# Loading the second half of the tokens behind the first quarter of the modulation, and accumulating half of its keys with the first half's

## The chip, the cores and the metric

The kernel runs on one core of one Trainium2 chip. The metric is the device time of one execution in microseconds; 1126.92 us is the median of three runs before the change.

## The reference

One layer of a diffusion backbone, in float32: 1024 latent tokens and 256 context tokens of width 1024. What matters here is its beginning. The modulation comes from the vector `c` (and `c_ctx` for the context) through the large matrix `w_mod`; the tokens are normalised, scaled and shifted with it, and then projected to keys, values and so on.

```python
mod_x = (jax.nn.silu(c) @ w_mod[l] + b_mod[l])[:, None, :]
mod_c = jax.nn.silu(c_ctx) @ w_mod[l] + b_mod[l]
sh1, sc1, gt1, sh2, sc2, gt2 = jnp.split(mod_x, N_MOD, axis=-1)
...
h_x = _modulate(x, g_pre_mix[l], sh1, sc1)    # rmsnorm(x, gain) * (1 + scale) + shift
h_c = _modulate(ctx, g_pre_mix[l], csh1, csc1)
u_x, q_x, k_x, v_x = _project(h_x, w_in[l])   # one matrix, four slices
u_c, q_c, k_c, v_c = _project(h_c, w_in[l])
attn_x = _neighbourhood_attention(q_x, k_x, v_x, k_c, v_c, rpb[l])
```

After that come the pooling mixer, the output projection and a squared-ReLU MLP, each with its own normalisation. They are the same before and after the change.

## The kernel before

**Numbers and tiles.** To keep float32's accuracy, every large product is made of three float32r matmuls: each operand is split into a high and a low part (`high_low`, `split` for weights, `modulated` for tokens), and `three` (L168 to L170) issues high by high, high by low, low by high. A page is a tile of 128 x 1024 float32, 512 KB; 33 of them are in the pool `pg`. A bank is a PSUM tile of 128 x 512; there are 8.

**The beginning.** The tokens are in two halves of 512, each in four pages with the tokens along the partitions: `xp` and `xq`. The 1024 columns of the width form eight blocks of 128, called k. For the keys, the columns must lie along the partitions, so each half is transposed by PE, block by block, into a bank (L289 for the first half, `turned`, L282, for the second). Of the modulation, shift and scale are needed here. `w_mod` is loaded in four quarters of two blocks each: four pages per quarter (`mod_load`, L244) beside one page of key weights (`wk0` to `wk3`, L148). For a quarter, `mod_rows` (L307) makes 16 matmuls that give its shift and scale as rows, which the trace shows as 32 pieces `pm`; ACT copies them, and `shift_scale` (L316, L320 to L322) turns them into columns, `a1` and `s1`.

With these, `latent(b, k, src)` modulates block k of half b, and `feature_group` adds block k to one of the key banks `pk{j}_{b}`: j counts four groups of 128 key features. A loop over the quarters q does this for the first half: modulate blocks 2q and 2q + 1 (ACT writes the high part, DVE the plain and the low one), twelve matmuls of block 2q, then the next quarter's weights and rows (`quarter(q + 1)`), then the twelve matmuls of block 2q + 1 with the next shift and scale between. In the last quarter the 16 transposes of the context (`pct`, L360) stand in place of the next rows.

**After the loop.** ACT modulates the context (`hc`, L175 and L176), copies the first half's keys out of their banks (L375), and then the second half of the tokens is normalised (`normalise("b", xq)`: squares on ACT, L130, the power -1/2 on POOL, L139, the scaling on DVE, L277). PE makes the context's keys in two groups of tokens (`pkc`); behind each group four blocks of the second half are transposed and modulated, here with `on_act=True`, where ACT writes the plain and the high part and DVE the low one. Then come all 96 matmuls of the second half's keys (8 blocks x 4 groups x 3), and their copies, L432. The value weights `wv` follow.

**What sets the order.** `in_order` ties the instructions of PE, ACT, DVE and SP in this part to the order in which they are written: no instruction of an engine passes an earlier one. All loads of the part are on SP's queue, in this order: the four pages of `xp`; per quarter one page of `wk` and four of `w_mod`; two pages of context, `cp`; four pages of `xq`. They are 26 pages, and no page of the pool is used twice among them. The value weights are released behind the last ACT and the last DVE instruction of the part (`issue_after`).

Of the kernel before, what the change touches and what calls it, by code (L numbers as in the profile page):

```python
# [17 lines left out]
P = 128  # L18
D = 1024
KT = D // P  # L20
# [59 lines left out]
def hybrid_block(ctx, tc, x, ctx_in, w_mod, b_mod, gp1, gp2, w_in, pool_w, rpb, w_out, w1, w2, vectors,  # L80
                 mask, edge, out):
    nc = tc.nc
# [9 lines left out]
    def cst(name, shape, dt=F32):  # L92
        return const.tile(shape, dt, tag=name, name=name)

    def sm(name, n, bufs=1):
        return small.tile([P, n], F32, tag=name.split("_")[0], name=name, bufs=bufs)

    def page(name, dt=F32):
        return act.tile([P, 1024], dt, tag="pg", name=name)
# [19 lines left out]
    xg, og = tiles(x), tiles(out)  # L119

    ident = cst("ident", [P, P])
# [7 lines left out]
    def mean_square(junk, src, ms):  # L129
        nc.scalar.activation(junk, src, AF.Square, scale=D ** -0.5, accum_out=ms)  # L130

    def rsqrt_of(name, ms, more=None):
        v = sm(f"v{name}", 1, 4)
        if more is None:
            nc.vector.tensor_scalar_add(v, ms, EPS)
        else:
            nc.vector.scalar_tensor_tensor(v, ms, EPS, more, add, add)  # L137
        r = sm(f"r{name}", 1, 4)
        nc.gpsimd.tensor_tensor(r, v, nhalf, ALU.pow)  # L139
        return r  # L140
# [5 lines left out]
    def load(name, src):  # L146
        raw = wraw.tile([P, 1024], F32, tag="raw", name=f"{name}w")
        nc.sync.dma_start(raw.rearrange("p (a b) -> p a b", b=src.shape[-1]), src)  # L148
        return raw

    def high_low(name, raw):
        hi = whl.tile([P, 1024], F32R, tag="hl", name=f"{name}h")
        lo = whl.tile([P, 1024], F32R, tag="hl", name=f"{name}l")
        split(raw, hi, lo)
        return hi, lo
# [4 lines left out]
    def pair(w, kk, c0, n):  # L160
        return w[2 * kk * P : (2 * kk + 2) * P, c0 : c0 + n].rearrange("(a p) f -> p a f", p=P)

    def wk(w, k, lo, c, n):
        return w[k // 2][lo][:, (k % 2) * 512 + c : (k % 2) * 512 + c + n]


    def three(ps, ahi, alo, bhi, blo, first, last, more=False):
        nc.tensor.matmul(ps, ahi, bhi, start=first, stop=False, skip_group_check=more)  # L168
        nc.tensor.matmul(ps, ahi, blo, start=False, stop=False, skip_group_check=more)  # L169
        nc.tensor.matmul(ps, alo, bhi, start=False, stop=last, skip_group_check=more)  # L170

    def modulated(tmp, name, src, scale, shift, hi, lo, n, on_act=False):
        h = tmp.tile([P, 512], F32, tag="t", name=f"{name}t")
        if on_act:
            nc.scalar.activation(h[:, :n], src, AF.Identity, bias=shift, scale=scale)  # L175
            nc.scalar.copy(hi, h[:, :n])  # L176
        else:
            nc.scalar.activation(hi, src, AF.Identity, bias=shift, scale=scale)
            nc.vector.tensor_scalar(h[:, :n], src, scale, shift, mul, add)
        nc.vector.tensor_tensor(lo, h[:, :n], hi.bitcast(F32), sub)  # L180
# [36 lines left out]
    with tc.tile_pool(name="ps1", bufs=8, space=PSUM) as ps1, tc.tile_pool(name="tmp1", bufs=3) as tmp:  # L217

        def bank(name):
            return ps1.tile([P, 512], F32, tag="mm", name=name)  # L220
# [14 lines left out]
        def token_tile(name, src):  # L235
            t = page(name)
            nc.sync.dma_start(t, src)
            return t


        def mod_load(q, kh, w):
            src = w_mod[:, w * D + q * 256 : w * D + (q + 1) * 256].rearrange("(h k p) f -> h p k f", p=P, h=2)
            t = page(f"wm{q}_{kh}_{w}")
            nc.sync.dma_start(t.rearrange("p (k f) -> p k f", k=4), src[kh])  # L244
            return t
# [3 lines left out]
        for q in range(4):  # L249
            raw_k.append(load(f"wk{q}", pair(w_in, q, 1024, 512)))  # L250
            wm.append([[mod_load(q, kh, w) for w in range(2)] for kh in range(2)])
        cp = [token_tile(f"c{i}", ctx_in[i * P : (i + 1) * P, :]) for i in range(2)]
        xq = [token_tile(f"x{m}", xg[m]) for m in range(4, 8)]


        nc.vector.tensor_scalar_add(b_sc, b_sc, 1.0)
# [11 lines left out]
        def normalise(name, pages):  # L268
            jk = page(f"jk{name}")
            rs = []  # L270
            for i, t in enumerate(pages + [None]):
                if t is not None:
                    ms = sm(f"ms{name}_{i}", 1, 4)
                    mean_square(jk, t, ms)
                    rs.append(rsqrt_of(f"t{name}_{i}", ms))
                if i:
                    nc.vector.tensor_scalar_mul(pages[i - 1], pages[i - 1], rs[i - 1])  # L277

        def turned(name, pages, k):
            pt = bank(name)  # L280
            for i, t in enumerate(pages):
                nc.tensor.transpose(pt[:, i * P : (i + 1) * P], t[:, k * P : (k + 1) * P], ident)  # L282
            return pt
# [29 lines left out]
        def shift_scale(q, mr):  # L313
            pt = bank(f"pmt{q}")
            for j in range(2):
                nc.tensor.matmul(pt[:, 4 * j : 4 * j + 4], mr[:, j * P : (j + 1) * P], pck, start=True, stop=True)  # L316
            pv = pt[:, :8].rearrange("p (j w v) -> p w v j", w=2, v=2)
            hs = slice(2 * q, 2 * q + 2)
            for v in range(2):
                nc.vector.tensor_tensor(a1[v][:, hs], pv[:, 1, v], b_sc[:, hs], add)  # L320
                nc.vector.tensor_tensor(a1[v][:, hs], a1[v][:, hs], g1c[:, hs], mul)
                nc.vector.tensor_tensor(s1[v][:, hs], pv[:, 0, v], b_sh[:, hs], add)  # L322
# [3 lines left out]
        def latent(b, k, src):  # L326
            h = page(f"hx{b}_{k}", F32R)
            modulated(tmp, f"hx{b}_{k}", src, a1[0][:, k : k + 1], s1[0][:, k : k + 1], h[:, :512], h[:, 512:], 512,
                      on_act=(b == 1))
            hx[b][k] = h  # L330

        def feature_group(ps, w, c, b, ks):
            for k in ks:
                h = hx[b][k]
                three(ps, wk(w, k, 0, c, P), wk(w, k, 1, c, P), h[:, :512], h[:, 512:], k == 0, k == KT - 1)


        wgt = []
        kT = [page(f"kT{j}") for j in range(4)]
        pks = [bank(f"pk{j}_0") for j in range(4)]  # L340
        def quarter(q):
            wgt.append(high_low(f"wk{q}", raw_k[q]))
            return mod_rows(q)

        shift_scale(0, quarter(0))
        for q in range(4):
            for k in (2 * q, 2 * q + 1):
                latent(0, k, xT[k])
            if q == 3:
                normalise("c", cp)  # L350
            for j in range(4):
                feature_group(pks[j], wgt, j * P, 0, (2 * q,))
            if q < 3:
                mr = quarter(q + 1)
            else:
                pct = [bank(f"pct{kk}") for kk in range(KT // 2)]
                for k in range(KT):
                    for i in range(2):
                        o = (k % 2) * 256 + i * P
                        nc.tensor.transpose(pct[k // 2][:, o : o + P], cp[i][:, k * P : (k + 1) * P], ident)  # L360
            for j in range(4):
                if j == 2 and q < 3:
                    shift_scale(q + 1, mr)
                feature_group(pks[j], wgt, j * P, 0, (2 * q + 1,))
        hc = []
        for k in range(KT):
            if k % 2 == 0:
                hp = page(f"hc{k}", F32R)
            o = (k % 2) * 512
# [1 line left out]
                      s1[1][:, k : k + 1], hp[:, o : o + 256], hp[:, o + 256 : o + 512], 256,  # L371
                      on_act=True)
            hc.append((hp[:, o : o + 256], hp[:, o + 256 : o + 512]))
        for j in range(4):
            nc.scalar.copy(kT[j][:, :512], pks[j])  # L375
        normalise("b", xq)

        rest = []

# [40 lines left out]
        for i in range(2):  # L420
            ps = bank(f"pkc{i}")
            token_group(ps, wgt, ctx_tok(i))
            nc.scalar.copy(kct[:, i], ps)

            for k in range(4 * i, 4 * i + 4):
                latent(1, k, turned(f"pxt1_{k}", xq, k))
        pks = [bank(f"pk{j}_1") for j in range(4)]
        for k in range(KT):
            for j in range(4):
                feature_group(pks[j], wgt, j * P, 1, (k,))  # L430
        for j in range(4):
            nc.scalar.copy(kT[j][:, 512:], pks[j])  # L432
        raw_v = [load(f"wv{kk}", pair(w_in, kk, 1536, 512)) for kk in range(KT // 2)]
        startup.close()
        with tc.issue_after(last[ET.Activation]), tc.issue_after(last[ET.DVE]):
            wgt = [high_low(f"wv{kk}", raw_v[kk]) for kk in range(KT // 2)]
# [22 lines left out]
        wgt = in_group("wu", 0)  # L459
# [58 lines left out]
        wgt = in_group("wq", 512)  # L518
# [161 lines left out]
    with tc.tile_pool(name="ps2", bufs=8, space=PSUM) as ps2:  # L680
# [4 lines left out]
      with ExitStack() as tmp2:  # L685
# [357 lines left out]
        with tc.issue_after(first[ET.PE]), in_order(ET.PE, ET.Activation, ET.DVE, ET.SP):  # L1043
# [59 lines left out]
            x = four("pyx")  # L1103
# [83 lines left out]
```

## Time and profile before

| | us |
|---|---|
| median of three runs | 1126.92 (1125.63 to 1127.53) |
| the profiled execution | 1126.66 |
| its span, from the first to the last instruction | 1124.9 |
| PE busy | 1075.7 |
| DVE busy | 696.4 |
| ACT busy | 511.1 |
| POOL busy | 61.6 |

The mean granted clock of TensorE is 0.985 of full speed. The page cuts the span into 40 slices of 28 us, and the part that the change touches is the first four. A matmul's length in the timeline includes its way through the array; matmuls that follow each other overlap, and the distance between starts is what one of them adds. Lines such as L168 are those of helpers, so a row is told apart by its tile: `pk` is a bank of latent keys, `pkc` of context keys, `pm` the modulation's rows, `pxt` transposed tokens, `pct` transposed context.

### The profile page before, as it was taken

How to read it: one execution, taken by the hardware profiler on the slowest of the kernel's cores; microseconds unless marked ns; L12 is line 12 of the kernel's file. 1: busy time of each engine (PE TensorE's matmuls, PEld its weight loads, DVE VectorE, ACT ScalarE, POOL GpSimd, SP SyncE). 2: the span in 40 equal slices, each digit the busy share in tenths (PEclk: the TensorE clock that was granted, in tenths of full speed). 3: DMA queues.
4: the chain of work that ended last, by engine and by line, in shares of the span. 5: the costliest groups of instructions: out<-in, count | busy, mean ns of one | idle time of the engine just before them, and what ended most of it. 6: DMA issues, size and time to landing. Idle time of an engine off the chain costs nothing.

```text
span 1124.9 us, 14398 instructions
## 1 busy us (share of the span) xinstructions
PE 1075.7 (96%) x5456; PEld 865.8 (77%) x5456; DVE 696.4 (62%) x1089; ACT 511.1 (45%) x848; POOL 61.6 (5%) x109
## 2 busy tenths in 40 slices
PE   5979999998999999998999999999999999999996
PEld 3667887785677778886888888888878888888885
DVE  4432654624788832579888767675477667556575
ACT  4373112313777732477555455554454334334441
POOL 1020000004220000220000000000000000000001
PEclk9989999998999999998999999999999999999998
DMA  9911863224000001852664535353587666555546
GB/s 285 312 50 37 276 231 113 92 95 143 20 20 2 5 16 48 240 172 75 217 212 165 186 127 173 130 173 112 208 322 277 252 244 223 180 194 187 188 172 202
DMA packets 94265, 179.32 MB, mean 159 GB/s; under 512 B 6898, under 2 KB 39154, under 8 KB 94196
## 3 DMA queue, kind: packets, MB, share of 16 engines
q1 hardware_dynamic: 76644, 144.80, 39.2%
q10 hardware_dynamic: 16272, 29.40, 7.0%
q0 software_dynamic: 1280, 4.21, 1.1%
q8 instruction: 43, 0.70, 0.3%
q14 instruction: 26, 0.21, 0.1%
HBM read 140.62 MB, written 37.76 MB: 159 GB/s over the span
## 4 chain that ended last, share of the span: by engine, by line
PE 83%; DVE 5%; ACT 4%; DMA 4%; issue 2%; POOL 2%; SPq 0%; ACTq 0%; DVEq 0%; POOLq 0%
PE S L586 3%; PE po L650 3%; PE pyv L170 3%; PE pyz L170 3%; PE pyz L169 3%; PE pyv L169 3%; PE pyv L168 3%; PE pyz L168 3%; PE T L624 3%; PE phz L170 3%; PE phz L168 2%; PE phz L169 2%; PE phv L170 2%; PE phv L168 2%; PE phv L169 2%; PE pyx L169 2%
## 5 line engine op out<-in xcount | busy, mean ns | idle before, releaser
L840 ACT ACTIVATE c<-c 128x512 f32<-128x512 f32 x48 | 30.4, 632 | 58.5 <-DVE c L938 24.0
L608 ACT ACTIVATE sp<-sp,nm 128x640 f32<-128x640 f32 (+1 forms) x64 | 51.5, 805 | 11.3 <-DVE nm L600 11.3
L168 PE MATMUL phx<-thB,wpA 128*128 128x512 f32 x128 | 51.1, 400 | 5.6 <-ACT s L898 5.6
L144 DVE TENSOR_TENSOR wpS<-S,wpS 128x512 fp32r<-128x512 f32 x64 | 43.7, 686 | 13.8 <-ACT wpS L143 13.8
L600 DVE CUSTOM_DVE_ANT_0 sp<-S,tab 128x640 f32<-128x640 f32 (+1 forms) x56 | 42.9, 802 | 14.3 <-PE S L586 14.3
L625 ACT COPY pt<-T 128x512 f32<-128x512 f32 x64 | 37.1, 579 | 31.1 <-PE T L624 27.9
L169 PE MATMUL phx<-tlB,wpA 128*128 128x512 f32 x128 | 50.7, 396 | 0.0
L170 PE MATMUL phx<-thB,wpA 128*128 128x512 f32 x128 | 50.5, 395 | 0.0
L143 ACT CAST wpS<-S 128x512 fp32r<-128x512 f32 x64 | 39.3, 615 | 23.3 <-PE phv L170 10.3
L624 PE MATMUL T<-ident,sp 128*128 128x128 f32 x256 | 37.1, 285 | 2.8 <-DVE px L631 2.7
L624 PEld LDWEIGHTS T<-ident,sp 128*128 128x128 f32 x256 | 28.1, 143 | 14.7 <-issue 7.3
L139 POOL TENSOR_TENSOR ry<-vy,nhalf 128x1 f32<-128x1 f32 x8 | 4.4, 550 | 612.1 <-DVE vy L137 612.1
L615 DVE TENSOR_SCALAR sp<-sp,ri 128x640 f32<-128x640 f32 (+1 forms) x64 | 35.4, 553 | 2.3
L586 PE MATMUL S<-kT,q 64*128 64x384 f32 (+1 forms) x128 | 31.9, 525 | 3.2 <-DVE nm L600 3.1
L841 ACT ACTIVATE c<-c 128x512 f32<-128x512 f32 x48 | 30.3, 632 | 10.0 <-DVE sa L911 9.2
L168 PEld LDWEIGHTS phx<-thB,wpA 128*128 128x128 f32 x128 | 24.6, 192 | 11.5 <-ACT s L898 6.4
L713 DVE TENSOR_TENSOR mp<-pw,Ga 128x512 f32<-128x512 f32 x16 | 11.0, 689 | 35.0 <-ACT jo L130 35.0
L946 DVE TENSOR_TENSOR c<-phz,u 128x512 f32<-128x512 f32 x16 | 11.1, 691 | 32.4 <-PE phz L170 32.4
L563 POOL TENSOR_TENSOR tab<-msk,U 128x128 f32<-128x128 f32 x48 | 24.8, 554 | 71.1 <-DMA U<-in_rpb 71.1
L170 PEld LDWEIGHTS phx<-thB,wpA 128*128 128x128 f32 x128 | 24.6, 192 | 5.3
L169 PEld LDWEIGHTS phx<-tlB,wpA 128*128 128x128 f32 x128 | 24.6, 192 | 5.1
L130 ACT ACTIVATE jo<-pw 128x512 f32<-128x512 f32 x16 | 9.6, 598 | 40.4 <-PE pw L170 40.4
(893 smaller groups left out, 3281.3 us busy)
## 6 DMA issues: line engine op xcount, KB each, us to landing
b<-in_w SPq DMA_DIRECT2D x64, 512.0 KB, 4.1
hrS<-hdS SPq DMA_DIRECT2D x32, 512.0 KB, 4.8
hrA<-hdA SPq DMA_DIRECT2D x24, 512.0 KB, 4.7
wm<-in_w_mod SPq DMA_DIRECT2D x16, 512.0 KB, 9.7
wa_0w<-in_w SPq DMA_DIRECT2D x16, 512.0 KB, 4.8
wa_1w<-in_w SPq DMA_DIRECT2D x16, 512.0 KB, 4.2
hdA<-c ACTq DMA_DIRECT2D x32, 256.0 KB, 2.1
hdS<-sa ACTq DMA_DIRECT2D x32, 256.0 KB, 2.9
```

The costliest lines, as they stand in the source:

```text
L143: nc.scalar.copy(hi, src)
L144: nc.vector.tensor_tensor(lo, src, hi.bitcast(F32), sub)
L168: nc.tensor.matmul(ps, ahi, bhi, start=first, stop=False, skip_group_check=more)
L169: nc.tensor.matmul(ps, ahi, blo, start=False, stop=False, skip_group_check=more)
L170: nc.tensor.matmul(ps, alo, bhi, start=False, stop=last, skip_group_check=more)
L586: nc.tensor.matmul(S[e][:, c0 : c0 + keys.shape[1]], q[hs, cols], keys[hs], start=True, stop=True)
L600: nc.vector.tensor_tensor_reduce(out=to, in0=s, in1=bt, scale=1.0, scalar=BIG, op0=add, op1=ALU.min, accum_out=nm)
L608: nc.scalar.activation(sp, sp, AF.Exp, bias=least[i, e], scale=-1.0, accum_out=su)
L615: nc.vector.tensor_scalar_mul(probs[i, e], probs[i, e], ri)
L624: nc.tensor.transpose(t[:, c * P : (c + 1) * P], probs[i, e][:, c * P : (c + 1) * P], ident)
L625: nc.scalar.copy(turns[i][0][:, e], t.rearrange("p (i t) -> p i t", i=4))
L650: nc.tensor.matmul(po[e * HD : (e + 1) * HD, (m % 4) * P : (m % 4 + 1) * P], v[:, f : f + HD], pt[:, e, c] if c < 4 else px[:, e], start=( ...
```

## The change

The four loads of `xq` are written behind the first quarter's five loads, ahead of the second quarter's. The second half is normalised in the first quarter. At the end of each quarter its two blocks of the second half are transposed, and in the next quarter they are modulated (`latent(1, k)`) and added to the banks of two of the four feature groups (`second_keys`: j = 0 and 1, twelve matmuls per quarter), so that six banks are held through the loop. Blocks 6 and 7 follow behind the loop, then the copies of the first half's keys, the last twelve matmuls of `second_keys`, and the context's transposes. The other two feature groups of the second half (j = 2 and 3, 48 matmuls) are accumulated after the context's modulation is issued, and the context's keys come last.

```diff
             wm.append([[mod_load(q, kh, w) for w in range(2)] for kh in range(2)])
+            if q == 0:
+                xq = [token_tile(f"x{m}", xg[m]) for m in range(4, 8)]
         cp = [token_tile(f"c{i}", ctx_in[i * P : (i + 1) * P, :]) for i in range(2)]
-        xq = [token_tile(f"x{m}", xg[m]) for m in range(4, 8)]
...
-        kT = [page(f"kT{j}") for j in range(4)]
-        pks = [bank(f"pk{j}_0") for j in range(4)]
+        pks = [[bank(f"pk{j}_{b}") for j in range(4 if b == 0 else 2)] for b in range(2)]
...
+        def second_keys(q):
+            for j in range(2):
+                feature_group(pks[1][j], wgt, j * P, 1, (2 * q, 2 * q + 1))
+
         shift_scale(0, quarter(0))
+        pxt = {}
         for q in range(4):
-            for k in (2 * q, 2 * q + 1):
+            ks = (2 * q, 2 * q + 1)
+            for k in ks:
                 latent(0, k, xT[k])
+            if q == 0:
+                normalise("b", xq)
+            else:
+                for k in (2 * q - 2, 2 * q - 1):
+                    latent(1, k, pxt[k])
             if q == 3:
                 normalise("c", cp)
             for j in range(4):
-                feature_group(pks[j], wgt, j * P, 0, (2 * q,))
+                feature_group(pks[0][j], wgt, j * P, 0, ks[:1])
+            if q:
+                second_keys(q - 1)
             if q < 3:
                 mr = quarter(q + 1)
-            else:
-                pct = [bank(f"pct{kk}") for kk in range(KT // 2)]
-                (the 16 transposes of cp)
             for j in range(4):
                 if j == 2 and q < 3:
                     shift_scale(q + 1, mr)
-                feature_group(pks[j], wgt, j * P, 0, (2 * q + 1,))
+                feature_group(pks[0][j], wgt, j * P, 0, ks[1:])
+            for k in ks:
+                pxt[k] = turned(f"pxt1_{k}", xq, k)
+        for k in (6, 7):
+            latent(1, k, pxt[k])
+        kT = [page(f"kT{j}") for j in range(4)]
+        for j in range(4):
+            nc.scalar.copy(kT[j][:, :512], pks[0][j])
+        second_keys(3)
+        pct = [bank(f"pct{kk}") for kk in range(KT // 2)]
+        (the 16 transposes of cp)
         hc = []
...
-        for j in range(4):
-            nc.scalar.copy(kT[j][:, :512], pks[j])
-        normalise("b", xq)
+        for j in range(2):
+            nc.scalar.copy(kT[j][:, 512:], pks[1][j])
+        pks = [bank(f"pk{j}_1") for j in (2, 3)]
+        for k in range(KT):
+            for j in (2, 3):
+                feature_group(pks[j - 2], wgt, j * P, 1, (k,))
+        for j in (2, 3):
+            nc.scalar.copy(kT[j][:, 512:], pks[j - 2])
...
             nc.scalar.copy(kct[:, i], ps)
-
-            for k in range(4 * i, 4 * i + 4):
-                latent(1, k, turned(f"pxt1_{k}", xq, k))
-        pks = [bank(f"pk{j}_1") for j in range(4)]
-        for k in range(KT):
-            for j in range(4):
-                feature_group(pks[j], wgt, j * P, 1, (k,))
-        for j in range(4):
-            nc.scalar.copy(kT[j][:, 512:], pks[j])
```

More of the change, by code (lines that the diff above doesn't have):

```diff
@@ L351, in hybrid_block @@
             for j in range(4):
-                feature_group(pks[j], wgt, j * P, 0, (2 * q,))
+                feature_group(pks[0][j], wgt, j * P, 0, ks[:1])
+            if q:
+                second_keys(q - 1)
             if q < 3:
                 mr = quarter(q + 1)
-            else:
-                pct = [bank(f"pct{kk}") for kk in range(KT // 2)]
-                for k in range(KT):
-                    for i in range(2):
-                        o = (k % 2) * 256 + i * P
-                        nc.tensor.transpose(pct[k // 2][:, o : o + P], cp[i][:, k * P : (k + 1) * P], ident)
             for j in range(4):
@@ L363, in hybrid_block @@
                     shift_scale(q + 1, mr)
-                feature_group(pks[j], wgt, j * P, 0, (2 * q + 1,))
+                feature_group(pks[0][j], wgt, j * P, 0, ks[1:])
[9 more added lines that the diff above has]
+        for k in range(KT):
+            for i in range(2):
+                o = (k % 2) * 256 + i * P
+                nc.tensor.transpose(pct[k // 2][:, o : o + P], cp[i][:, k * P : (k + 1) * P], ident)
         hc = []
@@ L373, in hybrid_block @@
             hc.append((hp[:, o : o + 256], hp[:, o + 256 : o + 512]))
-        for j in range(4):
-            nc.scalar.copy(kT[j][:, :512], pks[j])
-        normalise("b", xq)
+        for j in range(2):
+            nc.scalar.copy(kT[j][:, 512:], pks[1][j])
+        pks = [bank(f"pk{j}_1") for j in (2, 3)]
+        for k in range(KT):
+            for j in (2, 3):
+                feature_group(pks[j - 2], wgt, j * P, 1, (k,))
+        for j in (2, 3):
+            nc.scalar.copy(kT[j][:, 512:], pks[j - 2])
         rest = []
@@ L423, in hybrid_block @@
             nc.scalar.copy(kct[:, i], ps)
-            for k in range(4 * i, 4 * i + 4):
-                latent(1, k, turned(f"pxt1_{k}", xq, k))
-        pks = [bank(f"pk{j}_1") for j in range(4)]
-        for k in range(KT):
-            for j in range(4):
-                feature_group(pks[j], wgt, j * P, 1, (k,))
-        for j in range(4):
-            nc.scalar.copy(kT[j][:, 512:], pks[j])
         raw_v = [load(f"wv{kk}", pair(w_in, kk, 1536, 512)) for kk in range(KT // 2)]
```

## The prediction

> **What bounds the kernel now.** I read the page first: its busy shares, then its slices.
>
> ```profile
> span 1124.9 us, 14398 instructions
> PE 1075.7 (96%) x5456; PEld 865.8 (77%) x5456; DVE 696.4 (62%) x1089; ACT 511.1 (45%) x848; POOL 61.6 (5%) x109
> PEclk9989999998999999998999999999999999999998
> ```
>
> PE carries the kernel, and outside the beginning nothing is touched. The slices are 28 us each; the third has a lower clock, so something happens between 56 and 84 us. The waits of PE and PE's timeline there show what (start, length, then line, operation and tile; in brackets the idle time before and who ended it):
>
> ```profile
> PE pxt L282 <- DVE x L277: 5.8, 4, 3.1
> 64.33 0.39 PE L170 MATMUL pkc<-wk3h,hc 128*128 128x512 f32 x1
> 67.77 0.45 PE L282 MATMUL pxt<-ident,x 128*128 128x128 f32 x1 [3.05 <-DVE x L277]
> 71.92 3.04 PE L282 MATMUL pxt<-ident,x 128*128 128x128 f32 x13 [1.38 <-DVE x L277]
> 77.31 0.43 PE L168 MATMUL pkc<-wk1h,hc 128*128 128x512 f32 x1
> 81.44 1.91 PE L282 MATMUL pxt<-ident,x 128*128 128x128 f32 x16
> 83.58 0.23 PE pk L169
> ```
>
> The last row is from the chain that ended last: a 512-column matmul adds 0.23 us when PE is fed (the 0.39 of the timeline overlaps its neighbours). PE stops at 64.56 (64.33 + 0.23) because the second half of the tokens is normalised only then, behind the context's modulation on ACT. Full speed is back at 77.31. Of these 12.75 us, 16 transposes at full clock take 1.91 and six matmuls 1.38, so 9.5 us are lost. The windows say why it is more than the 5.8 us of waits (length; busy time of PE, PEld, DVE, ACT, POOL; granted clock; DMA share; GB/s):
>
> ```profile
> 2.00:11.00 9.00, 0.84 (x4) 0.85 (x5) 1.97 (x9) 3.69 (x7) 1.57 (x2) 1.00 1.00 234
> 19.90:27.30 7.40, 5.27 (x43) 3.32 (x42) 5.36 (x13) 3.13 (x5) 0.00 (x0) 1.00 1.09 356
> 41.50:43.50 2.00, 1.77 (x8) 1.47 (x9) 1.90 (x4) 1.10 (x2) 0.00 (x0) 1.00 1.04 408
> 43.70:52.70 9.00, 8.76 (x63) 6.02 (x62) 3.54 (x14) 4.09 (x7) 0.55 (x1) 1.00 1.04 239
> 63.72:67.14 3.42, 1.00 (x5) 0.50 (x3) 0.50 (x3) 3.36 (x7) 0.66 (x2) 1.00 0.00 0
> 67.14:77.38 10.24, 6.86 (x23) 5.43 (x24) 5.68 (x9) 7.24 (x13) 4.51 (x5) 0.50 0.01 2
> 265.11:268.52 3.41, 1.70 (x11) 0.83 (x9) 2.62 (x3) 1.62 (x3) 3.41 (x4) 1.00 0.83 269
> ```
>
> After a stretch with 1.00 us of PE work in 3.42 the clock fell to 0.50, for 10.24 us. A stretch with 1.70 in 3.41 elsewhere did not lower it.
>
> The first four rows are about transfers. The first half's tokens came at 234 GB/s. Loads of modulation and key weights run at 356 GB/s, the context's rows at 408, the second half's tokens at 239. PE's quarters leave little slack against them:
>
> ```profile
> x<-in_x SPq DMA_DIRECT2D x4, 512.0 KB, 14.2
> L244 SPq DMA_DIRECT2D wm<-in_w_mod x4: 706/1416/1417, 14.2 to 17.9; - x4
> DMA to landing us min/median/max: 9.4/9.4/9.4
> 26.72 0.39 PE L170 MATMUL pk<-hx,wk0l 128*128 128x512 f32 x1
> 27.04 1.93 PE L307 MATMUL pm<-wm,sT 128*32 128x256 f32 x32
> 28.90 0.50 PE L168 MATMUL pk<-hx,wk0h 128*128 128x512 f32 x1
> ```
>
> The second quarter's four modulation loads are issued from 14.2 to 17.9 us and land 9.4 later, the last at 27.3. PE starts their products at 27.04, with no wait. The beginning is thus limited by transfers up to about 27 us, by PE to 64, by ACT to 72, and by PE again.
>
> **The change part by part.** *The four token loads move ahead of the second quarter.* On SP's queue they are now ahead of wk1 to wk3, twelve modulation loads and the two context loads. They are 4 x 512 KB = 2.10 MB; at 239 GB/s, 8.8 us. Everything behind lands that much later: the first page of the second quarter at 14.2 + 9.4 + 8.8 = 32.4, the last at 27.3 + 8.8 = 36.1. PE's order is written out: after the first key's twelve matmuls come the 32 pieces of the second quarter's rows. Behind them stand the second key's products, shift and scale, and the new transposes; nothing may pass. PE is idle from 27.0 to 32.4, does the pieces of the first pages, and after 36.1 has 14 of the 32 left (the first piece that needs the last page is the third of the second half's sixteen): 14 x 1.93 / 32 = 0.8. They end at 36.9 instead of 28.9: **+8.0**. At the 234 GB/s of the first half's tokens it would be 9.0 and 8.2, so 8.0 to 8.2.
>
> The third and fourth quarter cost no wait: each needs five loads, 2.62 MB or 7.4 us at 356 GB/s, while PE's own quarter grows from 24 x 0.23 + 1.93 and shift and scale, some 8 us, by twelve matmuls (2.8) and eight transposes (1.0) to almost 12.
>
> *The clock.* With five idle microseconds, more than those that preceded 67.14, it must fall. It returns only after a stretch of unbroken work: the second half of the 10.24 us window, from 71.92 to 77.38, is 5.5 us of that. From 36.1 on I take 5.2 us at half clock, a loss of **+2.6**; bounds 1.7 (one 3.41 us stretch) and 5.1 (all of 10.24 after the restart). The Trainium skill's "TensorE: Matmul & The Clock Gate", Part 1, states that about 3.4 us of sustained work release the half-rate clock; by it this term would be 1.7 and the sum 0.9 lower. The row of 10.24 us speaks for more.
>
> *The normalisation of the second half* moves to the first quarter. ACT's squares, POOL's powers and DVE's scalings lie in the idle time before 36 us. The wait for it at L282 and its slow clock go: **-9.5**. If that cover were absent, its four squares (1.18 us each, by the spacing of 64.40, 65.61 and 66.79 below) would stand before the casts of wk1.
>
> ```profile
> 64.40 1.09 ACT L130 ACTIVATE jkb<-x 128x1024 f32<-128x1024 f32 x1
> 65.61 1.06 ACT L130 ACTIVATE jkb<-x 128x1024 f32<-128x1024 f32 x1
> 66.79 1.06 ACT L130 ACTIVATE jkb<-x 128x1024 f32<-128x1024 f32 x1
> 72.43 0.78 ACT L175 ACTIVATE hx_0t<-pxt,s,a 128x512 f32<-128x512 f32 x1 [2.84 <-PE pxt L282]
> 73.77 0.77 ACT L175 ACTIVATE hx_1t<-pxt,s,a 128x512 f32<-128x512 f32 x1
> 73.89 0.69 DVE L180 TENSOR_TENSOR hx<-hx_0t,hx 128x512 fp32r<-128x512 f32 x1 [2.03 <-ACT hx L176]
> 32.32 0.49 PE L168 MATMUL pk<-hx,wk1h 128*128 128x512 f32 x1
> 33.05 0.50 PE L169 MATMUL pk<-hx,wk1h 128*128 128x512 f32 x1 [0.23 <-DVE hx L180]
> 52.80 0.39 PE L170 MATMUL pk<-hx,wk3l 128*128 128x512 f32 x1
> 53.56 0.30 PE L360 MATMUL pct<-ident,c 128*128 128x128 f32 x1 [0.37 <-DVE c L277]
> 56.27 0.47 PE L168 MATMUL pk<-hx,wk3h 128*128 128x512 f32 x1
> 104.77 0.39 PE L170 MATMUL pk<-hx,wk3l 128*128 128x512 f32 x1
> 106.78 0.50 PE L168 MATMUL pvc<-wv0h,hc 128*128 128x512 f32 x1 [1.62 <-ACT wv0h L143]
> ```
>
> *Eight transposes at the end of each quarter* stand where PE now waits for the next modulated column: from 32.32 the second matmul starts after 0.73 us instead of 0.23. Three such waits go: **-1.5**. The transposes themselves are moved from 68 to 83 us, not added.
>
> *The context's transposes* move from inside the fourth quarter to behind its end, when the context has long been normalised. Now they fill 53.03 to 56.27, 3.24 us for 1.9 us of work: **-1.4**. Their four banks come from the first half's keys, whose ACT copies are over before the last second keys are.
>
> *Half of the second half's keys, inside the loop:* 36 of their 48 matmuls sit in quarters two to four, at no extra work. Their modulated columns need per quarter 2 x 1.34 us of ACT (72.43 to 73.77) behind the first half's; the second is ready about when PE arrives after its twelve matmuls, so 0 to 1.0 us in all, taken as 0.
>
> *The last twelve, second_keys(3),* have nothing in front: columns 6 and 7 can only be modulated once the transposes just before are done. From 72.43 to the end of the first low part at 74.58 is 2.15 us; the second follows 1.34 later, 3.5 in all. ACT starts about 0.3 before PE's last transpose ends, so PE has the last low part 3.2 after that end, then eight of its twelve matmuls (1.8): 5.0 instead of 2.8, **+2.3** (bounds 1.3, if only the first column's wait shows, and 2.9).
>
> *The rest:* six banks held instead of four, so the first rows wait for a later bank copy, and a key copy instead of four at the end, before the value weights (the 1.62 us wait at 106.78 stays): **+0.3**. The context's modulation on ACT comes to lie beside 48 matmuls, 11 us of second-half keys, and is hidden.
>
> Sum: 8.0 + 2.6 - 9.5 - 1.5 - 1.4 + 2.3 + 0.3 = +0.8 us; with all bounds together from -1.2 to +5.2. The profiled execution took 1126.66 us (span 1124.9 and 1.8 around it), so 1127.5; it lies 0.26 under the median of 1126.92, against which I forecast **1127.7**. What a measurement of this kernel can tell from no change is about 0.2%, 2.25 us; the forecast lies inside.
>
> **Rivals.** *Faster: the tokens come through sooner.* If the second half moves at the context's 408 GB/s, it takes 5.1 us instead of 8.8, the wait is 3.7 shorter, and the sum -2.9: 1124.0. For it speaks that their 4 KB rows are as long as the context's, and that a place between weight loads is a new one. Against it: 234 and 239 GB/s in both stretches in which tokens are loaded, whatever ran beside them. The Trainium skill's "DMA: Bandwidth & Descriptors", Where 436 GB/s comes from, puts the HBM side at about 358 GB/s; by that the loads would take 5.9 us and the sum be -2.1. The same page's Latency and other measured facts has rows a large power of two apart read at about 207, which is nearer to this trace's 239.
>
> *Slower: the clock falls a second time, at second_keys(3).* The 2.3 us of gaps come within some 3.2 us. Should they fall into one 3.41 us stretch, PE has 1.1 us of work in it, next to the 1.00 after which the clock fell and below the 1.70 after which it did not. That is where it decides. Half clock then costs between 1.7 and 5.1 us, taken as 3.4: +4.2, 1131.1. For it: the gap at L282 that let it fall had 3.05 us in one piece and more gaps behind it (1.38 at 71.92). Against it: the gaps here are split in four. The Trainium skill's "TensorE: Matmul & The Clock Gate", HAM oscillation, warns only of gaps longer than about 3.4 us; by that rule this rival is void and the sum stays at +0.8, but the trace disagrees, as a gap of 3.05 us brought half clock.
>
> *The move costs nothing:* if the second quarter's rows had 9 us to spare, the first two terms would go and the sum be -9.8: 1117.1. The row at 27.04 against a landing at 27.3 says there is no such slack; I give it nothing.
>
> **How the numbers follow.** Forecast 0.52: of it 0.40 within 0.2%, 0.10 slower by more (the upper bounds of clock and second-keys waits), 0.02 faster. Slower rival 0.27, faster rival 0.21. So faster 0.23, same 0.40, slower 0.37. Cases of both signs hold much; the forecast alone reaches from 1125.7 to 1132.1. The range runs from the faster rival with the low clock term (0.9 less) and half of what the second-keys wait could be shorter (0.5), 1122.6, to the slower one with 1.5 more at half clock, near its dearer bound: 1132.6.
>
> **What would show it.** In the changed profile PE's 32 pieces of the second quarter (pm, L307's counterpart) should be split, the last ending near 37 us behind a DMA wait, with clock 0.50 from about 30 to 41 us; tokens at about 239 GB/s between 19 and 28. No wait of PE for DVE's x near 65; gaps of about 2.3 us for hx just ahead of the context's transposes, near 80; pvc starting within 2 us of 107. A second 0.50 near 80 is the slower rival, tokens through by 25 us the faster one. The forecast is wrong if the second quarter's rows do not wait some 8 us, or if a wait of over 1 us stands in the later quarters.

## The result and the profile after

The changed kernel takes 1124.74 us (median of 22 runs, 1122.64 to 1129.06), the kernel before 1127.26 (22 runs, 1125.63 to 1128.38). The ratio is 0.9981, 95% interval 0.9974 to 0.9988: 2.1 us faster by the ratio (1.4 to 2.9), 2.5 by the medians. The forecast was +0.8. The time lies within the stated range, but the move went the other way, beyond the interval.

The profiled execution after took 1123.8 us. Its page:

```profile
span 1122.0 us, 14402 instructions
PE 1076.6 (96%) x5456; PEld 865.1 (77%) x5456; DVE 696.2 (62%) x1089; ACT 511.5 (46%) x848; POOL 61.9 (6%) x109
PEclk9999999998999999998999999999999999999998
```

PE is as busy as before. The low clock in the third slice is gone from this coarse view. Three of the six rows of PE's waits between 20 and 110 us bear on the change (who waited for whom; us in total, times, longest):

```profile
PE pm L308 <- DMA wm<-in_w_mod: 4.6, 4, 2.1
PE pvc L168 <- ACT wv0h L143: 1.6, 1, 1.6
PE pk L168 <- ACT hx L176: 1.1, 1, 1.1
```

PE's timeline around them:

```profile
31.38 0.62 PE L308 MATMUL pm<-wm,sT 128*32 128x256 f32 x2 [2.14 <-DMA wm<-in_w_mod]
32.89 2.56 PE L308 MATMUL pm<-wm,sT 128*32 128x256 f32 x16 [0.89 <-DMA wm<-in_w_mod]
35.89 1.37 PE L308 MATMUL pm<-wm,sT 128*32 128x256 f32 x14 [0.44 <-DMA wm<-in_w_mod]
37.19 0.50 PE L168 MATMUL pk<-hx,wk0h 128*128 128x512 f32 x1
72.96 1.03 PE L283 MATMUL pxt<-ident,x 128*128 128x128 f32 x8
75.08 0.50 PE L168 MATMUL pk<-hx,wk3h 128*128 128x512 f32 x1 [1.08 <-ACT hx L176]
80.41 2.17 PE L385 MATMUL pct<-ident,c 128*128 128x128 f32 x16
106.00 0.50 PE L168 MATMUL pvc<-wv0h,hc 128*128 128x512 f32 x1 [1.62 <-ACT wv0h L143]
```

The wait of 5.8 us for DVE's x at L282 is gone. In its place PE waits for the second quarter's modulation loads, in pieces; the last 14 pieces start at 35.89, where the prediction had the last page at 36.1, and the next matmul at 37.19 (predicted 36.9, before 28.90). The gaps ahead of `second_keys(3)` are there: between the transposes at 72.96 and the context's at 80.41 stand 7.45 us for some 3.6 us of work. The value weights start at 106.00 instead of 106.78. So in this pair of profiles the changed part gives only 0.8 us of the 2.9 by which the spans differ.

Windows of the profile after show the tokens' rate and where the clock was low (columns as in the prediction):

```profile
18.80:27.50 8.70, 5.72 (x27) 3.86 (x28) 5.34 (x15) 5.72 (x10) 1.46 (x2) 0.74 1.03 242
22.91:29.74 6.83, 5.79 (x12) 3.76 (x12) 3.94 (x9) 5.68 (x10) 2.56 (x3) 0.50 1.03 269
33.15:36.56 3.41, 2.97 (x24) 0.93 (x19) 0.00 (x0) 0.00 (x0) 0.00 (x0) 0.50 1.08 363
77.52:80.94 3.42, 3.42 (x11) 2.64 (x10) 0.00 (x0) 0.78 (x2) 0.00 (x0) 0.50 0.00 0
```

The tokens come at 242 GB/s at the new place. The clock is at half from 22.91 to 29.74, where PE does the twelve matmuls behind which it waits anyway, and from 33.15 to 36.56, where the pieces wait for the last page until 35.89. When the last page is there, the clock is back within 0.7 us. A second fall from 77.52 to 80.94 hits the last matmuls of `second_keys(3)`.

### The profile page after: what moved, and what is told of

It is laid out like the page before. It is cut to its first block, busy times and chain, and to the rows that moved or that the text cites. A ratio compares the mean times of both kernels' runs of the same rounds, so it can differ in the third digit from the quotient of the medians.

```text
span 1122.0 us, 14402 instructions
## 1 busy us (share of the span) xinstructions
PE 1076.6 (96%) x5456; PEld 865.1 (77%) x5456; DVE 696.2 (62%) x1089; ACT 511.5 (46%) x848; POOL 61.9 (6%) x109
## 4 chain that ended last, share of the span: by engine, by line
PE 85%; DMA 4%; ACT 3%; DVE 3%; issue 2%; POOL 1%; SPq 1%; DVEq 0%; POOLq 0%; ACTq 0%
PE S L603 3%; PE po L667 3%; PE pyv L169 3%; PE pyz L169 3%; PE pyv L168 3%; PE pyz L168 3%; PE pyv L170 3%; PE pyz L170 3%; PE T L641 3%; PE phz L168 3%; PE phz L169 3%; PE phz L170 3%; PE phv L168 2%; PE phv L169 2%; PE phv L170 2%; PE pyx L169 2%
## 5 line engine op out<-in xcount | busy, mean ns | idle before, releaser
L857 ACT ACTIVATE c<-c 128x512 f32<-128x512 f32 x48 | 30.3, 632 | 58.5 <-DVE c L955 24.1
L617 DVE CUSTOM_DVE_ANT_0 sp<-S,tab 128x640 f32<-128x640 f32 (+1 forms) x56 | 42.9, 801 | 13.2 <-PE S L603 13.2
L858 ACT ACTIVATE c<-c 128x512 f32<-128x512 f32 x48 | 30.3, 632 | 10.0 <-DVE sa L928 9.2
```

What stands on the lines that cost most here:

```text
L617: nc.vector.tensor_tensor_reduce(out=to, in0=s, in1=bt, scale=1.0, scalar=BIG, op0=add, op1=ALU.min, accum_out=nm)
```

## The experiments

A note on how they are read: "start" is the start of the value weights' first matmul (pvc), which ends the changed part; "behind" is the span less that, a stretch in which all kernels do the same work; "rows end" is the start of the first matmul behind the second quarter's 32 pieces.

**Loads alone.**

```diff
             wm.append([[mod_load(q, kh, w) for w in range(2)] for kh in range(2)])
+            if q == 0:
+                xq = [token_tile(f"x{m}", xg[m]) for m in range(4, 8)]
```

> The kernel before, with only the four loads of the second half moved behind the first quarter's; normalisation, transposes and keys stay where they were. Theory A (the move costs what its transfer takes, and the clock's fall lies inside the wait): the second quarter's rows end some 8 us later than 28.9 us, the wait at L282 stays, +8 us (7 to 9). Theory B (as the prediction had it, the clock stays at half for about 5 us after the wait): +10.6 us. Theory C (the tokens come through sooner at this place): at most +5 us.

Ratio 1.0068 (1.0055 to 1.0082), +7.7 us (6.2 to 9.2). Its waits of PE:

```profile
PE pxt L283 <- DVE x L278: 6.1, 4, 3.1
PE pm L308 <- DMA wm<-in_w_mod: 4.9, 4, 1.9
```

Both waits stand there, the old one untouched. That is theory A's size; theory B's 10.6 lies outside the interval, theory C's 5 too. In its one profile the second quarter's rows end at 37.46, and the clock is back at full before that, at 36.7.

**Order alone**, loads where they were:

```diff
-        for j in range(4):
-            nc.scalar.copy(kT[j][:, :512], pks[j])
         normalise("b", xq)
+        for j in range(4):
+            nc.scalar.copy(kT[j][:, :512], pks[j])
...
             nc.scalar.copy(kct[:, i], ps)
-            for k in range(4 * i, 4 * i + 4):
-                latent(1, k, turned(f"pxt1_{k}", xq, k))
+        pxt = [turned(f"pxt1_{k}", xq, k) for k in range(KT)]
+        for k in range(KT):
+            latent(1, k, pxt[k])
```

> The kernel before, loads where they were; the second half is normalised ahead of the copies of the first half's keys, both groups of context keys come first, and all 32 transposes and the eight modulations of the second half behind them. If the 9.5 us lost between 64.56 and 77.31 us come from the place of the normalisation alone: -9 us (-8 to -9.5), no half clock near 70. If the gain of the change needs the early loads: no more than -3 us, with a new wait of PE for ACT or DVE near 70.

Ratio 0.9897 (0.9883 to 0.9910), -11.6 us (-13.2 to -10.1), more than the -8 to -9.5 that were expected. All of PE's waits from 24 to 100 us:

```profile
PE pvc L168 <- ACT wv0h L143: 1.6, 1, 1.6
PE pct L360 <- DVE c L277: 1.2, 2, 0.8
PE pk L169 <- DVE hx L180: 0.9, 4, 0.2
```

A window from the last matmuls of the first half's keys to the start:

```profile
58.00:98.00 40.00, 38.64 (x187) 32.05 (x185) 12.62 (x23) 26.55 (x48) 8.07 (x10) 1.00 0.05 17
```

There is no wait at L282 and no half clock between 58 and 98 us; the 5.5 us of the second group of context keys now cover the normalisation. The start is at 98.26, 8.5 us earlier than in the first profile of the kernel before. The stretch behind, which the edit does not touch, is 1015.5 us here, the shortest of all profiles; so what goes beyond 9.5 us lies in that stretch. The stall at L282 was a matter of the order on ACT and PE alone, and its removal needs no early load.

**Transposes of blocks 6 and 7 earlier**, in the changed kernel:

```diff
+            if q == 3:
+                for k in ks:
+                    pxt[k] = turned(f"pxt1_{k}", xq, k)
             for j in range(4):
                 ...
                 feature_group(pks[0][j], wgt, j * P, 0, ks[1:])
-            for k in ks:
-                pxt[k] = turned(f"pxt1_{k}", xq, k)
+            if q < 3:
+                for k in ks:
+                    pxt[k] = turned(f"pxt1_{k}", xq, k)
```

> The changed kernel, with the transposes of blocks 6 and 7 ahead of the last twelve matmuls of the first half instead of behind them, so that these cover the modulation. If the gaps ahead of second_keys(3) cost what the prediction said: -2.3 us against the changed kernel, and up to -4 where the clock fell there; so -4.8 to -5.5 against the kernel before. If another wait takes their place: no difference from the changed kernel (-2.5 against before).

Ratio 0.9957 (0.9945 to 0.9970), -4.8 us against before, where the changed kernel has -2.1 by its ratio: 2.7 us between them (1.1 to 4.3 by the two intervals), near the 2.3 of the term. PE has no wait at all between 45 and 100 us, and the start moves to 103.41 (timeline):

```profile
71.73 1.03 PE L283 MATMUL pxt<-ident,x 128*128 128x128 f32 x8
78.08 1.91 PE L389 MATMUL pct<-ident,c 128*128 128x128 f32 x16
103.41 0.50 PE L168 MATMUL pvc<-wv0h,hc 128*128 128x512 f32 x1 [1.62 <-ACT wv0h L143]
```

**PE kept at work through the wait**, in the changed kernel:

```diff
+        def keep_warm(ps, n):
+            for i in range(n):
+                nc.tensor.matmul(ps, wk(wgt, 0, 0, 0, P), hx[0][0][:, :512], start=True, stop=True)
...
+            if q == 1:
+                spare = bank("spare")
+                keep_warm(spare, 24)
             for k in range(KT):
+                if q == 1 and k == KT // 2:
+                    keep_warm(spare, 9)
                 for w in range(2):
```

> The changed kernel with 24 more matmuls into an unused bank ahead of the second quarter's rows and 9 between their halves, so that PE works through the wait for the loads. Theory A (half clock there costs next to nothing, since it lies in the wait): -0.5 to +0.3 us against the changed kernel, -2 to -3 against before. Theory B (the clock costs 2.6 us behind the wait): -2.6 against the changed kernel, -5 against before.

Ratio 0.9986 (0.9976 to 0.9995), -1.6 us: not faster than the changed kernel. Its timeline:

```profile
35.82 2.37 PE L304 MATMUL spare<-hx,wk0h 128*128 128x512 f32 x9
38.12 1.07 PE L317 MATMUL pm<-wm,sT 128*32 128x256 f32 x16
39.12 0.50 PE L168 MATMUL pk<-hx,wk0h 128*128 128x512 f32 x1
```

and its window through the wait:

```profile
29.61:40.00 10.39, 10.39 (x68) 7.20 (x68) 2.81 (x4) 1.73 (x4) 1.01 (x1) 1.00 1.09 354
```

The clock stayed full through the wait, but the added matmuls outlasted the loads: the rows end at 39.12, 1.9 us after the 37.19 of the first profile. By the ratios it is 0.5 us slower than the changed kernel, uncertain by 1.3 either way. That leaves 1.4 us that the full clock gave back, with anything from 0.1 to 2.7 possible. So this run does not separate the two theories: its own cost is as large as what it was to save.

**The same two kernels again**, for more profiles (three more of the kernel before, four of the changed one).

> The kernel before once more, for a second profile. If the 2 us by which the two first profiles differ behind the changed part (value weights to the end: 1018.1 us before, 1016.0 after) are a matter of where the clock's steps of 3.41 us fall, this stretch should come out elsewhere within 1016 to 1019 us; if they belong to the kernels, at 1018.1 again.

> The changed kernel once more, for a second profile. If it is the steps of the clock: a second fall at second_keys(3) in one profile and not in another (value weights start at 104.3 us without it, at 106.0 with it), and the stretch behind anywhere from 1016 to 1019 us; if they belong to the kernels: 106.0 and 1016.0 again.

> As after_again, a third profile of the changed kernel: the second quarter's rows end between 36.9 and 39 us by the steps of the clock, and the value weights start between 104 and 106.5 us.

> The kernel before, a third profile. Ten profiles so far give the stretch behind the changed part as 1015.5 us and about 0.85 us more for each microsecond by which the clock's fall at the start of the attention comes later than 162 us after the value weights' first matmul. If this holds: the value weights start near 106.8 to 107.0 us, and the stretch lies on that line, anywhere from 1015.5 to 1018.5.

> As before_third. If the kernel before tends to the later end of that line, its fall comes 163.5 to 165.5 us after the value weights' start, as in its first two profiles (165.2, 163.8).

> The changed kernel, a fourth profile. If it tends to the earlier end of that line: the fall comes 162 to 163 us after the value weights' start, as in its first three (162.7, 162.9, 162.4), and the stretch is 1015.5 to 1016.6. If the place is drawn anew each time, any value up to 1018.5. The value weights start between 104.2 and 108.9, by whether the clock falls at second_keys(3) and how long it stays at half after the wait.

> A fifth profile of the changed kernel, with the same two expectations as after_fourth: the early end of the line (1015.5 to 1016.6) if it belongs to the kernel, any value up to 1018.5 if it is drawn anew.

| profile | rows end | start | behind | span |
|---|---|---|---|---|
| before | 28.90 | 106.78 | 1018.1 | 1124.9 |
| before_again | 30.25 | 106.99 | 1017.0 | 1124.0 |
| before_third | 30.35 | 108.33 | 1018.0 | 1126.3 |
| before_fourth | 30.27 | 108.33 | 1015.8 | 1124.1 |
| after | 37.19 | 106.00 | 1016.0 | 1122.0 |
| after_again | 36.99 | 104.22 | 1016.6 | 1120.8 |
| after_third | 38.27 | 108.92 | 1015.9 | 1124.8 |
| after_fourth | 37.98 | 106.45 | 1016.3 | 1122.7 |
| after_fifth | 37.20 | 106.06 | 1016.2 | 1122.3 |

The start expected for the kernel before, near 106.9, was missed twice. The reason stands in before_third: the clock was at half just after the first key's matmuls began, so that the second quarter's pieces came 1.45 us later than the 27.04 of the first profile, with no load to wait for. Its timeline and two of its windows:

```profile
28.49 1.93 PE L307 MATMUL pm<-wm,sT 128*32 128x256 f32 x32
```

```profile
24.46:27.87 3.41, 3.41 (x9) 2.67 (x9) 1.97 (x3) 0.60 (x1) 0.00 (x0) 0.50 1.08 361
270.22:283.87 13.65, 11.56 (x32) 6.27 (x32) 7.48 (x20) 6.08 (x14) 7.71 (x20) 0.50 0.24 84
```

Three of the four profiles of the kernel before have such an early half clock of 3.41 us; the one on which the prediction was built has none. In before_again the start is hardly later all the same, because the half clock at the stall of L282 lasted 6.83 us there, where the other three have 10.24:

```profile
69.41:76.24 6.83, 3.94 (x17) 3.31 (x17) 3.75 (x6) 3.93 (x7) 3.61 (x5) 0.50 0.01 3
```

The second window of before_third breaks the line on which the stretch behind was expected: the fall at the attention's start lasted 13.65 us there, not 10.24. The other three profiles of that round lie on the line, all at its early end; that was expected of the changed kernel if the early end belongs to it, but before_fourth has it too. The changed kernel's profiles differ as widely. Of after_third, a window and the timeline:

```profile
32.37:42.61 10.24, 8.94 (x43) 5.00 (x43) 1.78 (x8) 0.64 (x2) 0.00 (x0) 0.50 1.09 353
```

```profile
38.27 0.80 PE L168 MATMUL pk<-hx,wk0h 128*128 128x512 f32 x1
108.92 0.50 PE L168 MATMUL pvc<-wv0h,hc 128*128 128x512 f32 x1 [1.62 <-ACT wv0h L143]
```

Here the clock stayed at half for 4.3 us beyond the rows' end, much as the prediction had it, and fell again at `second_keys(3)`. The start, expected between 104 and 106.5, was later than in any profile of the kernel before. Of the 10.24 us, the middle step:

```profile
35.78:39.19 3.41, 2.97 (x17) 1.41 (x17) 0.00 (x0) 0.37 (x1) 0.00 (x0) 0.50 1.07 357
```

PE worked for 2.97 us in it, and half clock went on; in the first profile the step from 33.15, also with 2.97 us of work, ended it. So PE's busy time in a step does not tell when the clock comes back. In after_again, whose timeline follows, neither came, and it was at 104.22:

```profile
72.76 1.04 PE L283 MATMUL pxt<-ident,x 128*128 128x128 f32 x8
78.89 1.91 PE L385 MATMUL pct<-ident,c 128*128 128x128 f32 x16
104.22 0.50 PE L168 MATMUL pvc<-wv0h,hc 128*128 128x512 f32 x1 [1.62 <-ACT wv0h L143]
```

**A better order still?** order_only, with the context's 16 transposes moved:

```diff
             for j in range(4):
                 if j == 2 and q < 3:
                     shift_scale(q + 1, mr)
+                elif j == 2:
+                    (the 16 transposes of cp, which stood ahead of this loop)
                 feature_group(pks[j], wgt, j * P, 0, (2 * q + 1,))
```

> order_only with the context's transposes not ahead of the last twelve matmuls of the first half but between their two halves of six, so that the six cover the context's normalisation. If PE's wait of 1.2 us for the context simply goes: -1 us against order_only, -12 to -13 against the kernel before. If the context's modulation then comes too late for its keys: a new wait of PE for ACT near 59 us and no difference.

Ratio 0.9915 (0.9899 to 0.9932), -9.6 us, not the -12 to -13 of the first expectation; the interval overlaps that of order_only. The wait for the context is gone, but half of it comes back later, at the second half's transposes, which PE now reaches before the last page is scaled; first its wait, then its timeline:

```profile
PE pxt L282 <- DVE x L277: 0.6, 1, 0.6
```

```profile
97.89 0.51 PE L168 MATMUL pvc<-wv0h,hc 128*128 128x512 f32 x1 [1.62 <-ACT wv0h L143]
```

The start is 0.4 us earlier than in order_only, not 1. Which of the two is faster stays open; both beat the kernel before and the changed one.

**Shifting PE against the clock's steps**, in the changed kernel, behind the second half's last 48 matmuls (n = 4 or 12):

```diff
+        spare = bank("spare")
+        for i in range(n):
+            nc.tensor.matmul(spare, wk(wgt, 0, 0, 0, P), hx[1][0][:, :512], start=True, stop=True)
```

> The changed kernel with four more matmuls (0.9 us) into an unused bank, where PE works without a wait, between the second half's keys and the context's. Theory D (in the changed kernel PE leaves the beginning at a fixed place between the clock's steps, which decides how much of the half clock at the attention's start is spent waiting): the fall moves from 162.7 us after the value weights' start to 165.2, the stretch behind is 1018, and in all +2.8 us against the changed kernel, so about the same as the kernel before. Theory E (the place is drawn anew in each execution): +0.9 us, and a stretch anywhere from 1015.5 to 1018.5.

> The same with twelve more matmuls (2.7 us). Theory D: the fall comes at 163.4 us, the stretch behind is 1016.7, in all +3.2 us against the changed kernel, that is only 0.4 more than pad_4 although PE does 1.8 us more. Theory E: +2.7 us, 1.8 more than pad_4.

pad_4: ratio 0.9988 (0.9975 to 1.0001), -1.4 us; pad_12: 1.0003 (0.9990 to 1.0016), +0.3. Against the changed kernel's -2.1 these are +0.8 and +2.5, each uncertain by some 1.7: close to the 0.9 and 2.7 us of added work, but the +3.2 that theory D gives for pad_12 is possible too, and its +2.8 for pad_4 only just excluded. The stretch behind was 1015.6 in pad_4's profile (start 105.08) and 1018.6 in pad_12's (start 107.22), where theory D wanted 1018 and 1016.7. So both profiles speak against theory D, one for each pad; the times alone would not decide.

## Why the prediction was right or wrong

*The move of the loads (+8.0): right.* Alone it cost 7.7 us. In the profiles the rows end at 37.5 on average instead of 29.9: +7.6, with half clock on both sides of that difference. It would be 8.3 by the first profile of each.

*The tokens' rate: right*, 242 GB/s; the faster rival's condition did not come. That its 1124.0 lies close to the measured time is luck.

*The clock (+2.6): the step that failed.* It was argued that half clock would rest on PE for some 5 us after the last page. In three of five profiles it was over before the rows' end, in two it cost 1.2 and 2.0 us behind it (5.32 and 6.13 us from the rows' end to the next quarter's first matmul instead of 4.1): 0.65 us on average. Within the rows, the last 14 pieces took 0.99 us at full clock (after_again) and 1.49 on average: another 0.5. Together that is 1.2 us, less than the prediction's lower bound of 1.7. load_only, which excludes +10.6, says the same without the rest of the change.

Two things were overlooked. Half clock that lies on work behind which PE waits anyway costs nothing: the stretch from 22.91 to 29.74, which the prediction did not have at all, and much of the one from 33.15 to 36.56 are of this kind. And the 5.2 us were taken from one profile of one stall, as the unbroken work behind which the clock came back; in before_again the same stall needed 2.9 us (from PE's last wait there, which ends at 73.30, to 76.24). The changes of the clock come in steps of 3.41 us, and what decides at which step it returns is not shown, as the two steps with 2.97 us of work say.

*The profile as a yardstick: a second error.* The one profile of the kernel before had no early half clock; three later ones lose some 1.4 us to it (rows end at 30.3). In the changed kernel the same half clock costs nothing, as it lies ahead of the wait for loads. Over all profiles the start is 107.6 before and 106.3 after: -1.3 where the pair of first profiles says -0.8. Both differences are small against the scatter: the five starts of the changed kernel reach over 4.7 us, and the -1.3 has a standard error of 0.9.

*The wait at L282 (-9.5): right in size, wrong in what it needs.* order_only's start is 9.4 us earlier than the mean of the kernel before, without any early load. So this gain is not one of the early load, which by itself costs 7.7 us. *Eight transposes in place of three short waits (-1.5) and the context's transposes (-1.4)*: those waits are gone from the profile after; their sizes were not measured alone.

*second_keys(3) (+2.3): right.* Where the clock did not fall, 6.13 us stand between the two groups of transposes for 3.6 us of work: 2.5; turn_early gives back 2.7. *The slower rival happened,* in three of five profiles, but was priced too high: from the transposes at 72.96 and their like to the first matmul behind the context's transposes it is 9.36 or 9.37 us in those three and 7.80 in the other two, so 1.6 and not 3.4, since the fall comes in the middle of the last twelve matmuls and the clock is back after one step of 3.41 us. The sign by which it was to be decided was wrong too: a stretch with 1.70 us of work in 3.41 was taken as safe, but here the clock fell behind one with 1.99 (1.88 and 2.10 in the other two).

```profile
74.11:77.52 3.41, 1.99 (x6) 1.01 (x7) 1.38 (x2) 3.35 (x7) 1.29 (x2) 1.00 0.01 1
```

In these three falls the trace agrees with the half of the Trainium skill's rule ("TensorE: Matmul & The Clock Gate", Part 1) that gives 3.4 us of work as the price of the return: PE worked through the whole step, and full clock followed. It disagrees with its limit of about 3.4 us of idle time for the fall (HAM oscillation): gaps of 2.5 us in sum sufficed in three of five profiles.

The sum again, with what was measured: the clock at 1.2 instead of 2.6, 1.0 less for the early half clock of the kernel before, 0.9 more for the slower rival (1.6 in three of five) and 2.5 for `second_keys(3)` make -0.5 us over the changed part. (The prediction's bounds add up to -1.1 and +5.1, a tenth inside what it states.) The nine starts say -1.3, which their scatter does not tell from -0.5. Another 1 us of the measured 2.1 to 2.5 is left for the stretch behind, 1017.2 us on average in four profiles before and 1016.2 in five after. *That stays open,* and with it what made the sum come out negative: the changed part is about even, and which of these small terms tips it is not shown.

The stretch ranges from 1015.5 to 1018.6 over all 16 profiles. In 14 of them it lies within 0.3 us of the line that was expected for before_third, so the place of the clock's fall at the attention's start goes with nearly all of its changes; before_third and pad_12 lie 2.5 and 2.3 us above it. In all five profiles of the changed kernel that fall comes 162.4 to 162.9 us after the start, at the short end; in the kernel before at 161.9, 162.0, 163.8 and 165.2. That the changed kernel is tied to the short end was tried with the two pads, and they speak for chance; they do not exclude that a part is real.

## What to carry to other kernels

Moving a transfer ahead of another that PE is about to need cost nearly its whole duration here, 7.7 of 8.7 us, whatever it hides later; first see whether the late step is late because of its data or because of its place in an engine's order. Here the place was all of it: the order alone gives 9.6 to 11.6 us, the whole rearrangement 2.1. A stall's half clock should be priced only where PE would have something to do, and a difference of 2 us wants several profiles of both kernels before its terms are assigned.

## What the runs showed of the hardware

Within each of the 16 profiles all changes of the clock lie on one grid of 3.41 us. Where the grid lies differs from one execution to the next, and with it the start of the value weights moved within one kernel from 104.22 to 108.92 us. Half clock lasted 3.41, 6.83, 10.24 or 13.65 us, always whole steps, but for the last one, which the end of the program cuts off. PE's busy time in a step did not foretell a change: the clock fell behind a step with 1.99 us of work and not behind one with 1.70, and it came back after one step with 2.97 us and not after another. Token rows of 4 KB, 256 KB apart between groups of eight, came at 234 to 242 GB/s in three places, against 408 for the context's consecutive rows of the same length.
